# A gradient kernel on one core: part of the first tile loaded in separate pieces of 12 and 4 partitions

## The chip, the core and the metric

The kernel runs on one core of a Trainium2 chip; the other cores of the chip run nothing for it. The metric is the device time of one execution in microseconds (us), and the figure for a kernel is the median of its runs. The program is memory traffic with a little arithmetic: it reads 268.44 MB from the chip's main memory (HBM) and writes as much back. Between the two the data lie in the core's on-chip memory (SBUF), which has 128 partitions. Sixteen DMA engines move the data. VectorE (DVE) does the arithmetic, GpSimd (POOL) helps with the edges, and SyncE (SP) issues the transfers.

## What is computed

```python
def setup_inputs():
    return {"x": np.random.randn(8192, 8192).astype(np.float32)}

def reference(x):
    return np.gradient(x, axis=1)
```

Along each row of 8192 numbers, an inner element of the output is half the difference of its right and its left neighbour. The first element is x[1] - x[0] and the last is x[8191] - x[8190], both without the half.

## The kernel before

**Tiles.** `R = 2`, so one partition takes two consecutive rows, 2 x 8192 float32 numbers or 65,536 bytes that lie together in HBM. A tile is 128 partitions, or 256 rows and 8.39 MB, and there are `nsets = 32` tiles. `NB = 3` buffers called `slot0` to `slot2` hold tile i in slot i % 3. Each slot is 64 numbers (`SH`) longer than a tile: the load writes from column 64 on, and the result is written in place from column 0 on.

**One tile.** A load (line 60, one request of 128 x 16384 numbers) fills the slot. GpSimd computes the four edge differences of each partition into `ends` (line 70, 128 x 4). VectorE computes all inner differences in one instruction (line 76, 128 x 16382). The edges are then copied over the results (line 87), on GpSimd for tiles whose number leaves 1 or 3 when divided by 5, otherwise on VectorE. A store (line 89, again one request of 128 x 16384) writes the slot to HBM.

**Order.** The order is written out by hand. All 64 requests are issued by SP, one after the other: loads 0, 1, 2, then stores 0, 1, 2, loads 3, 4, 5, stores 3, 4, 5 and so on, to loads 30, 31, stores 30, 31. A store waits for the edge copy of its tile. Load i waits for the landing of store i - 3, which frees the slot. The function `chain` tells the framework that only these waits are needed. `loads` keeps the load instruction of each tile, so that the edge differences of tile i can be made to wait for it.

Of the kernel before, what the change touches and what calls it, by code (L numbers as in the profile page):

```python
# [1 line left out]

# [4 lines left out]


@with_exitstack
def kernel(  # L10
    ctx: ExitStack,
    tc: tile.TileContext,
    x: bass.AP,
    out: bass.AP,
):

    nc = tc.nc
    P = nc.NUM_PARTITIONS
    n, m = x.shape
    R = 2
    NB = 3  # L30
    SH = 64
    W = R * m
    nsets = n // (P * R)
    f32 = x.dtype

    x_sets = x.rearrange("(s p t) m -> s p (t m)", p=P, t=R)
    out_sets = out.rearrange("(s p t) m -> s p (t m)", p=P, t=R)

    pool = ctx.enter_context(tc.tile_pool(name="pool", bufs=1))
    slots = [pool.tile([P, SH + W], f32, name=f"slot{k}", tag=f"slot{k}") for k in range(NB)]  # L40
    ends = pool.tile([P, nsets, R, 2], f32, name="ends", tag="ends")
    loads, stores = [], [None] * nsets
    in_front = {}

    def chain(i, ins, *needed):

        group, engine = f"slot{i % NB}", ins.ins.engine
        keep = [o.ins for o in needed]  # L50
        if in_front.get(engine, (None,))[0] == group:
            keep.append(in_front[engine][1])
        tc.declare_no_dep(ins.ins, group=group, keep=keep, reason="implied by the needed step")
        tc.add_to_no_dep_group(group, ins.ins)
        in_front[engine] = group, ins.ins
        return ins

    def load(i):
        b = slots[i % NB]
        ins = nc.sync.dma_start(out=b[:, SH : SH + W], in_=x_sets[i])  # L60
        loads.append(chain(i, ins, *([stores[i - NB]] if i >= NB else [])))

    with tc.manual_schedule():
        for i in range(NB):
            load(i)
        for i in range(nsets):
            b = slots[i % NB]
            xin = b[:, SH : SH + W].rearrange("p (t m) -> p t m", m=m)

            ins = nc.gpsimd.tensor_sub(  # L70
                out=ends[:, i, :, :],
                in0=xin[:, :, 1 : m : m - 2],
                in1=xin[:, :, 0 : m - 1 : m - 2],
            )
            at = [chain(i, ins, loads[i])]
            ins = nc.vector._custom_dve(  # L76
                dve_ops.TENSOR_TENSOR_REDUCE_SUB_MAX,
                out=b[:, 1 : W - 1],
                in0=b[:, SH + 2 : SH + W],
                in1=b[:, SH : SH + W - 2],  # L80
                s0=0.0,
                s1=0.5,
            )
            halved = chain(i, ins, *at)
            res = b[:, 0:W].rearrange("p (t m) -> p t m", m=m)
            placer = nc.gpsimd if i % 5 in (1, 3) and i < nsets - 2 else nc.vector
            ins = placer.tensor_copy(out=res[:, :, 0 : m : m - 1], in_=ends[:, i, :, :])  # L87
            placed = chain(i, ins, halved)
            ins = nc.sync.dma_start(out=out_sets[i], in_=b[:, 0:W])
            stores[i] = chain(i, ins, placed)  # L90
            if i % NB == NB - 1:
                for k in range(i + 1, min(i + 1 + NB, nsets)):
                    load(k)


# [1 line left out]
_INS = ['x']  # L97
_OUTS = [((8192, 8192), 'float32')]


# [23 lines left out]
```

## Time and profile before

| | us |
|---|---|
| median of three runs | 1248.04 |
| lowest and highest of them | 1247.85, 1248.38 |
| span of the profiled execution, first to last instruction | 1245.7 |
| VectorE busy in it | 554.6 (45%) |
| GpSimd busy in it | 8.8 (1%) |

The profile is one execution. Its span leaves out what lies before the first and after the last instruction, which is why it is 2.3 us below the median of the runs. Three kinds of view are used here: the page's totals; the waits (which engine waited for what, and for how long in total); and a list of instructions in order of time, where a row of SP stands for a request that it issues and not for the transfer itself.

The trace also has a record of each packet that the DMA engines moved: its start, how long it took and how many bytes it had. There are 8192 data packets of 65,536 bytes, which is one partition of one tile each, and 1024 packets of 4 bytes, which tell the program that an engine has finished its part of a request. That is 128 data packets and 16 such marks for each of the 64 requests, so each engine moves 8 data packets and one mark per request. The records do not name the engine. Since a packet starts within a few ns of the end of the one before it on its engine, the sixteen streams can be followed as groups: the records in order of start, sixteen at a time, are called rounds here, and round 0 is the first packet of each engine.

### The profile page before, as it was taken

What the parts mean: (1) busy time and instruction counts of PE and PEld (TensorE: products, weight loads), DVE (VectorE), ACT (ScalarE), POOL (GpSimd) and SP (SyncE); (2) the same over time, 40 slices, a digit from 0 to 9 for tenths busy, and PEclk for the clock granted to TensorE, in tenths of its full rate; (3) what the DMA queues carried; (4) which work ended last, traced back from release to release, by engine and by line L of the source; (5) the groups of instructions that cost most, each with busy time, mean ns of one, the idle gap of its engine ahead of it and who ended that gap; (6) DMA issues with size and microseconds to landing.
All of it is one profiled execution on the core that took longest, in us unless ns stands there. A gap on an engine that the chain in (4) does not pass through costs nothing.

```text
span 1245.7 us, 237 instructions
## 1 busy us (share of the span) xinstructions
DVE 554.6 (45%) x52; POOL 8.8 (1%) x48
## 2 busy tenths in 40 slices
DVE  2850583069009702850582079009603840591083
POOL 0000000000000000000000000000000000000000
DMA  9999999999999999999999999999999999999999
GB/s 404 438 436 423 427 431 438 438 438 436 436 427 431 425 438 436 425 434 436 429 434 436 434 436 434 436 434 438 419 436 436 434 438 438 431 434 429 429 410 404
DMA packets 9217, 536.88 MB, mean 431 GB/s; under 512 B 1024, under 2 KB 1024, under 8 KB 1024
## 3 DMA queue, kind: packets, MB, share of 16 engines
q1 hardware_dynamic: 9216, 536.88, 99.8%
q14 instruction: 1, 0.01, 0.0%
HBM read 268.44 MB, written 268.44 MB: 431 GB/s over the span
## 4 chain that ended last, share of the span: by engine, by line
another core or an unknown queue 74%; DVE 18%; DMA 3%; issue 2%; POOL 1%; SPq 0%; POOLq 0%
DVE slot L76 18%; DMA slot<-in_x_dram 3%; POOL ends L70 0%; POOL slot L87 0%; SPq L60 0%; POOLq L119 0%; DVE slot L87 0%
## 5 line engine op out<-in xcount | busy, mean ns | idle before, releaser
L76 DVE CUSTOM_DVE_ANT_0 slot<-slot 128x16382 f32<-128x16382 f32 x32 | 551.2, 17224 | 668.7 <-POOL ends L70 668.7
L70 POOL TENSOR_TENSOR ends<-slot 128x4 f32<-128x4 f32 x32 | 6.3, 198 | 989.6 <-DMA slot<-in_x_dram 989.6
L87 POOL COPY slot<-ends 128x4 f32<-128x4 f32 x12 | 2.3, 190 | 207.9 <-DVE slot L76 207.9
L87 DVE COPY slot<-ends 128x4 f32<-128x4 f32 x20 | 3.4, 172 | 0.7
L108 POOL MEMSET const-bfloat16-1.0<- 128x1 bf16 x1 | 0.1, 101 | 0.0
L108 POOL MEMSET const-uint8-127<- 128x1 uint8 x1 | 0.1, 101 | 0.0
L108 POOL MEMSET const-float32-0.0<- 128x1 f32 x1 | 0.1, 98 | 0.2 <-issue 0.2
L108 POOL MEMSET const-float32-1.0<- 128x1 f32 x1 | 0.1, 98 | 0.0
## 6 DMA issues: line engine op xcount, KB each, us to landing
slot<-in_x_dram SPq DMA_DIRECT2D x32, 58.0
out_dram<-slot SPq DMA_DIRECT2D x32, 40.4
```

The lines of the kernel that those rows point to most:

```text
L70: ins = nc.gpsimd.tensor_sub(out=ends[:, i, :, :], in0=xin[:, :, 1 : m : m - 2], in1=xin[:, :, 0 : m - 1 : m - 2],)
L76: ins = nc.vector._custom_dve(dve_ops.TENSOR_TENSOR_REDUCE_SUB_MAX, out=b[:, 1 : W - 1], in0=b[:, SH + 2 : SH + W], in1=b[:, SH : SH + W - 2],
L87: ins = placer.tensor_copy(out=res[:, :, 0 : m : m - 1], in_=ends[:, i, :, :])
L108: nc = _bacc.Bacc("TRN2", target_bir_lowering=False, num_devices=1)
```

## The change

Of the first tile alone, the load is cut into four requests. All other loads, and all stores, stay as they are.

```diff
+    EVEN, CUT = P - 16, m - 2048
+
+    def parts_of(dram, i, sb, last):
+        whole = dram.rearrange("(s p t) m -> s p t m", p=P, t=R)[i]
+        rows = sb.rearrange("p (t m) -> p t m", m=m)
+        cuts = [(slice(EVEN, P), slice(0, CUT))]
+        first = EVEN
+        for k in last:
+            cuts.append((slice(first, first + k), slice(CUT, m)))
+            first += k
+        pairs = [(whole[p, :, c], rows[p, :, c]) for p, c in cuts]
+        pairs.insert(1, (dram.rearrange("(s p t) m -> s p (t m)", p=P, t=R)[i][0:EVEN], sb[0:EVEN]))
+        return pairs
...
     def load(i):
-        b = slots[i % NB]
-        ins = nc.sync.dma_start(out=b[:, SH : SH + W], in_=x_sets[i])
-        loads.append(chain(i, ins, *([stores[i - NB]] if i >= NB else [])))
+        sb = slots[i % NB][:, SH : SH + W]
+        after = [stores[i - NB]] if i >= NB else []
+        parts = parts_of(x, i, sb, (12, 4)) if i == 0 else [(x_sets[i], sb)]
+        loads.append(
+            [chain(i, nc.sync.dma_start(out=to, in_=of), *after) for of, to in parts]
+        )
...
-            at = [chain(i, ins, loads[i])]
+            at = [chain(i, ins, *loads[i])]
```

SP now issues for tile 0, in this order:

1. partitions 112 to 127, columns 0 to 6143 of each of their two rows (16 x 2 x 6144 numbers, pieces of 24,576 bytes);
2. partitions 0 to 111, whole (112 x 16384 numbers, pieces of 65,536 bytes);
3. partitions 112 to 123, columns 6144 to 8191 (12 x 2 x 2048 numbers, pieces of 8,192 bytes);
4. partitions 124 to 127, columns 6144 to 8191 (4 x 2 x 2048 numbers, pieces of 8,192 bytes).

Together they move the same 8.39 MB into the same places. The edge differences of tile 0 wait for all four. No other instruction of any engine changes its place; line numbers from there on are higher by five.

## The prediction

> **What bounds the kernel now.** I read the page's totals first, then the waits, then the list of instructions at both ends.
>
> ```profile
> span 1245.7 us, 237 instructions
> DVE 554.6 (45%) x52; POOL 8.8 (1%) x48
> DMA  9999999999999999999999999999999999999999
> DMA packets 9217, 536.88 MB, mean 431 GB/s; under 512 B 1024, under 2 KB 1024, under 8 KB 1024
> q1 hardware_dynamic: 9216, 536.88, 99.8%
> ```
>
> The DMA engines are busy in every slice, 99.8% of the span; VectorE works less than half of it. Of the 8192 data packets, median, 5th and 75th percentile all took 2418 ns, so one packet time is 2418 ns and the 512 packets of one engine need 1238.0 us. Only 7.7 us of the span are anything else.
>
> ```profile
> POOL ends L70 <- DMA slot<-in_x_dram: 989.6, 32, 77.4
> DVE slot L76 <- POOL ends L70: 668.7, 32, 60.2
> ...
> SPq L60 <- DMA out_dram<-slot: 373.1, 29, 19.3
> ```
>
> GpSimd waits for loads, VectorE for GpSimd, and SP, before a load, for the store that frees the slot. Nothing here waits for arithmetic at the DMA's cost, as the two ends show:
>
> ```profile
> 0.74 1.33 SPq L60 DMA_DIRECT2D slot<-in_x_dram  x3
> 22.71 0.20 POOL L70 TENSOR_TENSOR ends<-slot 128x4 f32<-128x4 f32 x1 [22.27 <-DMA slot<-in_x_dram]
> 22.95 17.22 DVE L76 CUSTOM_DVE_ANT_0 slot<-slot 128x16382 f32<-128x16382 f32 x1 [22.95 <-POOL ends L70]
> 40.20 0.17 DVE L87 COPY slot<-ends 128x4 f32<-128x4 f32 x1
> 40.40 40.06 SPq L89 DMA_DIRECT2D out_dram<-slot  x3
> ...
> 1187.17 17.22 DVE L76 CUSTOM_DVE_ANT_0 slot<-slot 128x16382 f32<-128x16382 f32 x1 [59.84 <-POOL ends L70]
> 1204.42 0.17 DVE L87 COPY slot<-ends 128x4 f32<-128x4 f32 x1
> 1204.62 19.69 SPq L89 DMA_DIRECT2D out_dram<-slot  x2
> 1206.28 0.20 POOL L70 TENSOR_TENSOR ends<-slot 128x4 f32<-128x4 f32 x1 [19.14 <-DMA slot<-in_x_dram]
> ```
>
> Store 0 is issued at 40.40 us, but load 2 keeps the engines until 60.4 or later (its last packets begin at 57.95 to 58.54): 20 us of cover. At the end there is none. Tile 30's arithmetic starts when the slowest engine has landed load 30 (round 488, which follows it, begins at 1183.62 us on the fastest engine and at 1185.92 on the slowest), store 30 follows 17.5 us later, and all engines start it together (round 496, 1205.47 to 1205.84). So the end is set by **the slowest of sixteen engines**: a delay of the fast ones costs nothing there, a delay of the slowest moves the end one for one.
>
> What made that engine slow? Its second packet began at 5.39 us; 487 more would have put it at 1182.96, and it was 2.96 us later. The losses lie almost all in one place: the last packet of a load before the engines turn to stores. At the first turn the sixteen packets took 3162 to 3819 ns, 1.10 us over the usual on average (17.6 us summed over 16). The nine later turns cost 0.01 to 0.63 us on average, mean 0.23. Meanwhile the engines drift apart, from 0.6 us at the start to 2.3 near the end.
>
> **The change part by part.** *Issuing.* SP issues six requests at the start instead of three, three more at 0.34 us (median of 339 ns): load 1 leaves SP about 1.0 us later. Its packets are due at 21.7 us, so some 18 us of cover remain; without it the cost would be 1.0 us. The first request starts as before, 1.0 us after issue, and has 48 KB for each engine, 1.8 us at the usual rate; the second is issued 0.42 us after it and arrives before that is done. *Waits.* The edge differences of tile 0 wait for four landings instead of one; behind them on GpSimd is tile 1's, behind those VectorE, behind it store 0 with its 20 us. SP's requests take completion semaphores in turn, and three more requests shift that turn; what a later request then waits for is a request eight places earlier, long landed. I price both at nothing.
>
> *More and smaller packets.* One whole partition per engine becomes pieces of 24 and 8 KB, with 32 more marks, two per engine at 9 ns: 0.02 us. A start-up cost per new request is between nothing (queued packets follow each other within a few ns) and 0.60 us, the mean excess of the very first packets: for the three added requests 0 to 1.8 us. The queued packets are nearer, so 0.
>
> *Unequal shares.* A partition's last 2048 columns of two rows are 16 KB, a quarter of a packet: 0.60 us. If 12 engines take one partition each of request 3 and four of those again one of request 4, four engines carry 0.60 us more than before and four 0.60 less. If request 4 falls on the four left out, all shares are equal and this is 0. I take +0.60 on the slowest. [...]
>
> *Crowding.* Before, each request spreads 16 engines over 128 partitions. Now request 1 puts all sixteen into 16 neighbouring partitions, request 3 twelve into 12, request 4 four into 4, and request 2's seven partitions per engine no longer divide as eight do. No row shows so narrow a request. From below the cost is 0: all packets keep their rate. From above I let the whole first tile, eight packet times, go at the pace of the worst packet in the trace: 8 x (3819 - 2418) = 11.2 us. The first turn is the one place where all sixteen engines are seen in each other's way while they write SBUF; I hold that nearer than undisturbed streaming, and take its mean: 8 x 1.10 = **+8.8 us**. Nothing hides it, since the engines have no idle time to lend and each later request queues behind. [...]
>
> *The first turn.* Engines that are further apart could be spared part of it. From nothing to all of the slowest engine's 2.96 us; I take the first turn falling to the mean of the others, 1.10 - 0.23 = -0.9.
>
> Sum: 0.60 + 8.8 - 0.9 = +8.5 us. Span 1245.7 + 8.5 = 1254.2; with the 2.3 us between span and median, **1256.5 us**. Upper end: 0.60 + 11.2 + 1.8 = +13.6, 1261.6; with crowding at half my value, +4.1 or 1252.1. That is the likeliest case's own range.
>
> **The rivals.** *Only the shares count.* Narrow requests run at full rate, and the slowest engine carries 0.60 us more, or 0 if shares come out equal: 1248.0 to 1248.6, less up to 0.9 at the first turn. For it: ordinary packets keep to 2418 ns within a few ns through nearly all of the trace. Against: they do so with every engine on its own eight of 128 partitions.
>
> *The stagger pays, faster.* Place: the turns from loads to stores. The first cost 1.10 us with the engines 0.6 us apart; the turn at 291 us, with 1.2 us between them, 0.08, and the one at 988 us, with 2.4, 0.01. A spread of 1.2 us or more from the start could spare the slowest engine up to 2.96 us, less whatever extra share it has: 1245.1, or 1245.7 with the full share. It decides if crowding costs less than it spares; below 2.96 - 0.60 = 2.4 us it wins. Against: the turn at 522 us cost 0.63 with the engines 1.8 us apart, so spread alone does not spare a turn.
>
> *A starved start.* If the four requests come too slowly from SP, all engines idle up to 1.0 us between them: 1249.0. The 1.8 us of work in request 1 speaks against it.
>
> **How the numbers follow.** Crowding 0.70, at 1256.5. Shares only, with the starved start, 0.18, around 1248.5. Stagger 0.12, around 1245.5. What this kernel's measurement tells from no change is about 0.2%, 2.5 us: below 1245.5 or above 1250.5. Crowding gives slower but for 0.02; shares only gives no change; of the stagger 0.09 lies beyond the bound, where nearly all turns are spared. So slower 0.68, same 0.23, faster 0.09. The range for 8 in 10 starts at 1247.0, which leaves out the stagger, and ends at 1262.0, just over the upper sum.
>
> **What would show it.** The packets of q1 should number 9296 (48 more data packets, 32 more marks). Right, if the first edge difference starts near 32 us instead of 22.71, tile 0's pieces run far above the time for their bytes, and the 9 us last to the end of the trace. Only the shares, if it starts near 23.5 and the sixteen packet streams are 1.2 us apart with all turns as before. Stagger, if the first turn's excess falls from 1.10 below 0.3 and round 488's slowest start comes before 1185.9. I am wrong above all if narrow requests run at full rate: then 8.8 us of my sum are not there.

## The result, and the profile after

The changed kernel takes 1268.18 us (1267.89 to 1268.99) against 1248.04 for the kernel before, measured beside it: a ratio of 1.0162, 95% interval 1.0149 to 1.0174. It is 20.1 us slower. I had forecast slower, 1256.5 us, with 1262.0 as the upper end. The direction and its cause were right, and the size was less than half of what it is.

The page of the changed kernel, first its totals and then the three lines of its transfer list that stand for requests 1, 3 and 4 of tile 0 (kilobytes, and where it is given the us from issue to landing; request 2 is counted with the other loads):

```profile
span 1266.4 us, 245 instructions
DVE 554.6 (44%) x52; POOL 8.9 (1%) x48
DMA  9999999999999999999999999999999999999999
GB/s 219 337 433 431 431 435 428 437 441 431 439 433 433 431 431 433 437 424 447 431 439 435 431 431 428 433 433 445 433 433 437 428 433 435 433 431 443 433 391 397
DMA packets 9297, 536.88 MB, mean 424 GB/s; under 512 B 1056, under 2 KB 1056, under 8 KB 1056
q1 hardware_dynamic: 9296, 536.88, 99.6%
...
slot<-in_x_dram SPq DMA_DIRECT2D x1, 768.0 KB, 9.9
...
slot<-in_x_dram SPq DMA_DIRECT2D x1, 192.0 KB
slot<-in_x_dram SPq DMA_DIRECT2D x1, 64.0 KB
```

The busy row is the same as before, nines throughout: the engines are occupied all the time. The row of GB/s tells what that hides. Each slice is 31.7 us; the first moves data at half the later rate (219 GB/s against 433), the second at three quarters (337), and from the third on the kernel runs as before. A packet counts as busy for as long as it takes, so the slice at 219 GB/s shows the same nine as those at 433. The packets number 9296, as worked out, and 99.6% of the engines' time went into them.

The same stretches in both kernels, before and then after (start and end of the stretch, its length, VectorE's and GpSimd's busy time, the clock, the DMA's busy share, GB/s; a packet is counted whole where it starts, so short stretches are rough):

```profile
0.00:10.00 10.00, 0.00 (x0) 0.20 (x4) 1.00 0.98 400
10.00:40.00 30.00, 17.05 (x1) 0.20 (x1) 1.00 0.98 426
40.00:46.00 6.00, 4.07 (x3) 0.20 (x1) 1.00 0.88 382
...
62.00:100.00 38.00, 17.40 (x2) 0.20 (x1) 1.00 0.96 416
```

```profile
0.00:10.00 10.00, 0.00 (x0) 0.20 (x4) 1.00 1.15 184
10.00:40.00 30.00, 0.00 (x0) 0.00 (x0) 1.00 0.94 223
40.00:46.00 6.00, 0.00 (x0) 0.00 (x0) 1.00 0.88 259
...
62.00:100.00 38.00, 34.26 (x4) 0.59 (x3) 1.00 1.01 436
```

Request 2, the 112 whole partitions, fills the stretch from 10 to 40 us at 223 GB/s. The rows of the instructions in order of time show where that goes:

```profile
0.73 4.06 SPq L65 DMA_DIRECT2D slot<-in_x_dram  x6
46.15 0.20 POOL L75 TENSOR_TENSOR ends<-slot 128x4 f32<-128x4 f32 x1 [45.70 <-DMA slot<-in_x_dram]
...
65.16 0.20 POOL L75 TENSOR_TENSOR ends<-slot 128x4 f32<-128x4 f32 x1 [18.81 <-DMA slot<-in_x_dram]
...
84.51 0.20 POOL L75 TENSOR_TENSOR ends<-slot 128x4 f32<-128x4 f32 x1 [1.64 <-DMA slot<-in_x_dram]
...
1207.51 0.20 POOL L75 TENSOR_TENSOR ends<-slot 128x4 f32<-128x4 f32 x1 [77.08 <-DMA slot<-in_x_dram]
```

Each row of GpSimd starts 0.07 to 0.16 us after the last mark of a load has landed (45.99, 65.09, 84.44 and 1207.44 us): loads 0, 1, 2 and 30. Before, load 0's row stood at 22.71 us, and these are the other three:

```profile
42.04 0.20 POOL L70 TENSOR_TENSOR ends<-slot 128x4 f32<-128x4 f32 x1 [19.13 <-DMA slot<-in_x_dram]
...
62.44 0.20 POOL L70 TENSOR_TENSOR ends<-slot 128x4 f32<-128x4 f32 x1 [2.69 <-DMA slot<-in_x_dram]
...
1186.93 0.20 POOL L70 TENSOR_TENSOR ends<-slot 128x4 f32<-128x4 f32 x1 [77.07 <-DMA slot<-in_x_dram]
```

So the kernel is 23.4 us late after load 0, 23.1 after load 1, 22.1 after load 2 and 20.6 at load 30. Nothing more is lost after load 0 has landed; on the contrary, 1.0 us comes back at the first turn from loads to stores and 1.5 us after it. The span grew by 20.7 us.

The packet records give the rates. Typical ones of the changed kernel's first tile:

```
request 1, second pieces (24,576 bytes):    about 3600 ns each, usual rate 907 ns
request 2, first three packets (65,536):    about 4770 ns each after the start, usual rate 2418 ns
request 2, fourth and fifth:                about 3050 and 3560 ns on most engines
request 2, sixth and seventh:               about 4550 and 4770 ns, the last up to 5529
requests 3 and 4 (8,192 bytes):             600 to 1010 ns each, usual rate 302 ns
```

Sixteen engines at 24,576 bytes in 3600 ns are 109 GB/s, a quarter of the usual 434 (65,536 bytes in 2418 ns). Request 1 lasted from 2.26 to 9.3 us, request 2 from there to between 38.6 and 41.9 us, engine by engine. The first packets of load 1 that start beside the tail are slow too, up to 6033 ns.

### The profile page after: what moved, and what is told of

It is laid out like the page before. It is cut to its first block, busy times and chain, and to the rows that moved or that the text cites. A ratio compares the mean times of both kernels' runs of the same rounds, so it can differ in the third digit from the quotient of the medians.

```text
span 1266.4 us, 245 instructions
## 1 busy us (share of the span) xinstructions
DVE 554.6 (44%) x52; POOL 8.9 (1%) x48
## 3 DMA queue, kind: packets, MB, share of 16 engines
q1 hardware_dynamic: 9296, 536.88, 99.6%
## 4 chain that ended last, share of the span: by engine, by line
another core or an unknown queue 74%; DVE 18%; DMA 3%; issue 2%; POOL 1%; SPq 0%; POOLq 0%
DVE slot L81 18%; DMA slot<-in_x_dram 3%; POOL ends L75 0%; POOL slot L92 0%; SPq L65 0%; POOLq L124 0%; DVE slot L92 0%; POOLq L75 0%
```

## The experiments

Two theories stood against each other. **Crowding:** the set of partitions that a request covers sets its rate. **Pieces:** the number of requests and the small pieces cost. A third, **shares,** puts the loss on the unequal shares. In all the kernels below only tile 0 is loaded otherwise, unless said; the edits are shortened, with numbers in place of names, and a line without a condition holds for tile 0 alone.

**Whole partitions in two requests** (112 to 127, then 0 to 111):

```diff
-        parts = parts_of(x, i, sb, (12, 4)) if i == 0 else [(x_sets[i], sb)]
+        parts = [(x_sets[i][112:128], sb[112:128]), (x_sets[i][0:112], sb[0:112])] if i == 0 else [(x_sets[i], sb)]
```

> Tile 0 is loaded in two requests of whole partitions, 112 to 127 and then 0 to 111: no column cut, equal shares. Theory (which partitions a request covers sets its rate, as in the changed kernel, where 16 partitions went at 109 GB/s and 112 began at 220): 1.05 MB at 109 GB/s is 9.6 us instead of 2.4, and 112 partitions again need some 30 us instead of 17, so the first edge difference starts at 42 to 47 us and the time is 1263 to 1269 us. Rival (small pieces and the number of requests): there are none here but one request more, so it starts before 25 us and the time is within 2 us of the kernel before.

Measured: 1268.53 us, ratio 1.0162 (1.0142 to 1.0182); tile 1's edge difference at 62.90 us, and the first one here:

```profile
43.92 0.20 POOL L83 TENSOR_TENSOR ends<-slot 128x4 f32<-128x4 f32 x1 [43.48 <-DMA slot<-in_x_dram]
```

There are no small pieces and no unequal shares here, and the time is that of the changed kernel; at load 1, 20.9 of its 23.1 us are there. Pieces and shares are out as its main cause.

**More pieces over all partitions:**

```diff
+        parts = [(x_sets[i][:, c:d], sb[:, c:d]) for c, d in [(0, 6144), (6144, 8192), (8192, 14336), (14336, 16384)]]
```

> Tile 0 is loaded in four requests that each cover all 128 partitions: pieces of 24 and 8 KB by columns, more small pieces than in the changed kernel, equal shares. Theory (partitions covered): full rate, the first edge difference starts at 22.7 to 24 us, time within 1.5 us of the kernel before, the first turn still costs about 1 us per engine. Rival (small pieces and requests): much of the 20 us, over 1255 us.

Measured: 1248.50 us, ratio 1.000 (0.9991 to 1.0010). Its first rows:

```profile
22.78 0.20 POOL L82 TENSOR_TENSOR ends<-slot 128x4 f32<-128x4 f32 x1 [22.34 <-DMA slot<-in_x_dram]
...
42.04 0.20 POOL L82 TENSOR_TENSOR ends<-slot 128x4 f32<-128x4 f32 x1 [19.07 <-DMA slot<-in_x_dram]
```

Four requests with 512 pieces of 24 and 8 KB land tile 0 within 0.1 us of one request. With every request over all 128 partitions, the cut cost 0.0 us at load 1, which stands at 42.04 us in both kernels. The first turn cost 1.09 us per engine, as in the kernel before.

**Two halves of 64 partitions:**

```diff
+        parts = [(x_sets[i][0:64], sb[0:64]), (x_sets[i][64:128], sb[64:128])]
```

> Tile 0 is loaded in two requests of 64 whole partitions each, both with equal shares and large pieces. Theory: each half runs at about 220 GB/s, so the tile takes 38 us instead of 19.3, the first edge difference starts near 41.5 us, time 1264 to 1268 us. Rival that only awkward divisions (112, 12, 4) are slow: no change, 1247 to 1249 us.

Measured: 1267.82 us, ratio 1.0156 (1.0136 to 1.0177), with the first edge difference at 44.15 us:

```profile
44.15 0.20 POOL L83 TENSOR_TENSOR ends<-slot 128x4 f32<-128x4 f32 x1 [43.71 <-DMA slot<-in_x_dram]
```

Nothing divides awkwardly here, and it is as slow as the changed kernel. So it is not the odd numbers 112, 12 and 4.

**The disputed cost by itself.** The kernel before, with nine extra loads ahead of it into the third buffer, one after the other; their data are loaded again by the ordinary load 2. Each entry gives the first partition, the end and the step:

```diff
+        probes = [probe(*p) for p in [(0, 128, 1), (0, 16, 1), (0, 64, 4), (0, 128, 8), (0, 32, 1), (0, 128, 4), (0, 64, 1), (0, 112, 1), (0, 96, 1)]]
```

> Before the first tile, nine extra loads of whole partitions (65,536 bytes each) into a buffer, each waiting for the one before: 128 partitions; 16 neighbours; 16 in steps of 4; 16 in steps of 8; 32 neighbours; 32 in steps of 4; 64; 112; 96 neighbours. Theory (places decide): packets take 2.42 us in the 128, about 9.6 us for 16 neighbours, about 4.8 us for 16 in steps of 4 or of 8, for 32 and for 64; 112 starts at 4.8 us per packet. Rival (only the number of partitions decides): the three kinds of 16 take the same time. Rival (no such limit on an idle machine): 2.4 us everywhere. The time is longer by the sum of the extra loads, 110 to 160 us by the theory.

Measured in one run: 1401.42 us. The stretches from issue to issue of the first eight, in the order of the list (same columns as above; each holds about 2 us of waiting for the landing):

```profile
0.73:22.59 21.86, 0.00 (x0) 0.00 (x0) 1.00 0.92 384
22.59:34.22 11.63, 0.00 (x0) 0.00 (x0) 1.00 0.75 90
34.22:41.60 7.38, 0.00 (x0) 0.00 (x0) 1.00 0.65 142
41.60:49.42 7.82, 0.00 (x0) 0.00 (x0) 1.00 0.62 134
49.42:61.79 12.37, 0.00 (x0) 0.00 (x0) 1.00 0.81 170
61.79:69.45 7.66, 0.00 (x0) 0.00 (x0) 1.00 0.71 274
69.45:92.24 22.79, 0.00 (x0) 0.00 (x0) 1.00 0.88 184
92.24:125.71 33.47, 0.00 (x0) 0.00 (x0) 1.00 0.92 219
```

The second, third and fourth row move the same 1.05 MB on 16 partitions. Sixteen neighbours take 11.63 us, sixteen in steps of 4 or 8 only 7.38 and 7.82. The fifth and sixth row move the same 2.1 MB: 32 neighbours take 12.37 us, 32 in steps of 4 take 7.66. From the first packet's start to the last one's end the rates are:

| partitions | GB/s | median packet, ns |
|---|---|---|
| 128 | 409 | 2419 |
| 16 neighbours | 107 | 8678 |
| 16 in steps of 4 | 190 | 4721 |
| 16 in steps of 8 | 178 | 4822 |
| 32 neighbours | 198 | 5117 |
| 32 in steps of 4 | 348 | 2474 |
| 64 neighbours | 202 | 5119 |
| 112 neighbours | 230 | 4681 |
| 96 neighbours | 206 | 5005 |

Both rivals fall: neither the number of partitions alone decides (16 of them ran at 107, 190 and 178 GB/s), nor is the limit missing on an idle machine (409 GB/s on 128, but 230 on 112). What decides is which partitions a request covers: 32 in steps of 4 ran at 348 GB/s, 32 neighbours at 198. More neighbours help little from there on: 64 ran at 202, 96 at 206, 112 at 230. Why, no run here shows. In every kernel here a partition also stands for its own stretch of 65,536 bytes in HBM, so the runs alone do not tell whether the crowding lies on the SBUF side or on the HBM side.

**Equal shares in the tail** (16 partitions in one request in place of 12 and 4):

```diff
-        parts = parts_of(x, i, sb, (12, 4)) if i == 0 else [(x_sets[i], sb)]
+        parts = parts_of(x, i, sb, (16,)) if i == 0 else [(x_sets[i], sb)]
```

> As the changed kernel, but the last 2048 columns of partitions 112 to 127 come in one request of 16 instead of 12 and 4, so shares are equal. Theory (crowding makes nearly all of the loss): load 0 lands at 44 to 47 us as in the changed kernel, time within 2 us of its 1268.2. Rival (unequal shares are what costs): the time falls by more than 3 us. If the larger distance between the engines spared the later turns, this kernel's slowest engine loses 2.5 us between load 2 and load 30, as in the kernel before, and not 1.0 as in the changed one.

Measured: 1267.70 us, ratio 1.0161 (1.0147 to 1.0175). Tile 1's edge difference:

```profile
63.43 0.20 POOL L75 TENSOR_TENSOR ends<-slot 128x4 f32<-128x4 f32 x1 [18.83 <-DMA slot<-in_x_dram]
```

It came at 65.16 in the changed kernel, so 12 and 4 cost 1.7 us more than 16 at that point. At load 30 the order is reversed in the profiles, 1208.25 against 1207.51; but the profiled run of this kernel was the slowest of its four, at 1269.02 us, and by the medians it is not the slower one. Between load 2 and load 30 its slowest engine lost 3.5 us. (That loss is the time between the two edge differences, less 58 requests of 8 packets at 2418 ns, 1121.95 us.)

**The narrow tail alone** (a wide request for three quarters of the tile):

```diff
+        parts = [(x_sets[i][p, c], sb[p, c]) for p, c in [(slice(0, 128), slice(0, 12288)), (slice(0, 112), slice(12288, 16384)), (slice(112, 124), slice(12288, 16384)), (slice(124, 128), slice(12288, 16384))]]
```

> Tile 0: the first 12288 numbers of all 128 partitions in one request, then the last 4096 (16 KB) of partitions 0 to 111, 112 to 123 and 124 to 127 apart. A quarter of the changed kernel's crowded bytes, the same unequal shares and the same number of requests. Theory: 1.8 MB of 112 partitions at 230 GB/s is 8.0 us instead of 4.2, the 12 and the 4 add 1 to 3.6 us, so load 0 lands 5 to 7.5 us later than in the kernel before, time 1251 to 1256 us. Rival (requests that leave out partitions cost by themselves, whatever their bytes): 1262 us or more.

Measured: 1253.38 us, ratio 1.0045 (1.0031 to 1.0058), with the first edge difference 7.5 us later than before and tile 1's 7.2 later:

```profile
30.20 0.20 POOL L82 TENSOR_TENSOR ends<-slot 128x4 f32<-128x4 f32 x1 [29.76 <-DMA slot<-in_x_dram]
```

A quarter of the crowded bytes costs about a third of the changed kernel's 23.1 us. With four requests in both, the loss went with the crowded bytes here, not with the requests.

**Unequal shares without neighbours:**

```diff
+        parts = [(x_sets[i][r:128:4], sb[r:128:4]) for r in range(3)] + [
+            (x_sets[i][3:128:4, 0:12288], sb[3:128:4, 0:12288]),
+            (x_sets[i][3:96:4, 12288:16384], sb[3:96:4, 12288:16384]),
+            (x_sets[i][99:128:4, 12288:16384], sb[99:128:4, 12288:16384])]
```

> Tile 0 in six requests of 32 partitions in steps of 4 (the kind that ran at full rate in the measurement of nine loads), of which the last 16 KB of every fourth partition are cut into 24 and 8 partitions, so that shares are unequal without neighbours being crowded. Theory: load 0 lands 0 to 3 us later than the 22.6 us of the kernel before, first packets of each request near 2.4 us; time 1247 to 1251 us. Rival (any cut of the partitions is slow): 1260 us or more. If unequal shares alone are worth something, it is below 1247.

Measured: 1248.87 us, ratio 1.0008 (0.9999 to 1.0017). Its rows for loads 0, 1, 2 and 30:

```profile
25.59 0.20 POOL L85 TENSOR_TENSOR ends<-slot 128x4 f32<-128x4 f32 x1 [25.14 <-DMA slot<-in_x_dram]
...
44.66 0.20 POOL L85 TENSOR_TENSOR ends<-slot 128x4 f32<-128x4 f32 x1 [18.88 <-DMA slot<-in_x_dram]
...
64.01 0.20 POOL L85 TENSOR_TENSOR ends<-slot 128x4 f32<-128x4 f32 x1 [1.64 <-DMA slot<-in_x_dram]
...
1187.71 0.20 POOL L85 TENSOR_TENSOR ends<-slot 128x4 f32<-128x4 f32 x1 [77.10 <-DMA slot<-in_x_dram]
```

It is 2.6 us late at load 1, 1.6 at load 2 and 0.8 at load 30: of the 2.6 us, 1.8 come back. After the first packets of the kernel, the requests of 32 in steps of 4 ran at 2418 ns a packet. This is the change's idea without its neighbours, and it is a draw, not a gain.

**Why the first turn was free.** In the kernel before, the engines lose 1.10 us each when they first turn from loads to stores; in the kernels with a slow tile 0 they lose nothing there (0.00 to 0.01 us).

```diff
+        probes = [probe(*p) for p in [(0, 128, 1)]]
```

> The kernel before with one more full load of 128 partitions in front, into the third buffer, which is loaded again later: all else is 19.3 us later. It asks why the first turn to stores cost 1.1 us per engine in the kernel before and nothing in those with a slow first tile. If it is the engines' distance, or the slow tile itself, the first turn still costs about 1.1 us here and the time is 1248.2 + 19.3 + 0 = 1267.5 us. If it is that the first turn comes early after the start, it costs under 0.3 us and the time is about 1266.5 us.

Measured in one run: 1267.57 us, and the first turn cost 0.83 us. That it comes early after the start is not the reason.

```diff
+        parts = [(x_sets[i][r:128:4], sb[r:128:4]) for r in range(4)]
```

> Tile 0 in four requests of 32 whole partitions in steps of 4, equal shares, no column cut. If the first turn is spared because engines are at unequal distances (2.2 us apart with the unequal shares in steps of 4), it costs about 1.1 us per engine here, since the engines stay 0.5 to 0.8 us apart, and the time is within 0.6 us of the kernel before. If any division other than one request of 128 spares it, it costs under 0.1 us and the time is about 1247.0 us.

Measured: 1248.39 us, ratio 1.0006 (0.9997 to 1.0015), first turn 0.89 us, with the engines 0.9 us apart at load 1. It is 0.6 us late at load 1, so 2.0 of the 2.6 us of the unequal cut in steps of 4 belong to its tail. Cutting the tile in steps of 4 does not spare the turn, while the same cut with unequal shares, 2.2 us apart, did.

The two kernels as they are, profiled a second time:

> The changed kernel, profiled a second time. If what it gives back between load 2 and load 30 belongs to the change, the slowest engine loses about 1.0 us there again, the first turn is free again and load 30 lands 20 to 21 us later than in the kernel before; if it was chance, that loss lies anywhere between 1.0 and 3.1 us.

> The kernel before, profiled a second time. If its first turn belongs to it, it costs about 1.1 us per engine again, and the slowest engine loses about 2.5 us between load 2 and load 30; if these were chance, the first turn differs by more than 0.3 us.

Measured: the changed kernel, 1268.27 us, with load 1's edge difference at 65.00 us and load 30's at 1207.18; the kernel before, 1247.95 us, with a first turn of 1.05 us. Side by side, the slowest engine's loss between load 2 and load 30:

| kernel | shares in tile 0 | loss, us |
|---|---|---|
| before, twice | equal | 2.5, 2.9 |
| nine extra loads ahead | equal | 2.5 |
| one extra load ahead | equal | 3.2 |
| two whole requests | equal | 2.8 |
| four by columns | equal | 3.1 |
| two halves | equal | 2.6 |
| equal tail of 16 | equal | 3.5 |
| steps of 4, equal | equal | 2.5 |
| changed kernel, twice | unequal | 1.0, 0.9 |
| wide body, narrow tail | unequal | 1.6 |
| steps of 4, unequal | unequal | 1.7 |

Each figure is one profile, and the runs of the kernel before alone lie more than 2 us apart (1246.58 to 1249.32). Still every kernel with unequal shares lost less than every one with equal shares, and the changed kernel did so twice: on its slowest engine the unequal shares go with 1 to 2 us less. Whether they spare turns is not shown. Averaged over the sixteen engines, the nine later turns cost about as much in the kernel of two whole requests (equal, about 1.0 us in all) as in the changed one; it may also be that the same losses fall on engines that are ahead. For the first turn the distance between the engines is not the whole story: the two halves left them only 0.3 us apart at loads 1 and 2 and still turned free. Nor is a slow tile 0: after the nine extra loads, tile 0 came in one ordinary request, the engines were 0.9 us apart as with the equal steps of 4, and that turn was free. What decides it stays open; it was not pursued, since it is 1 us of 20.

## Why the prediction was wrong

*The bound.* Right. The end is set by the slowest DMA engine, and a delay in tile 0 goes through to the end: 23.1 us at load 1, 20.6 at load 30, 20.7 in the span. No wait on an engine took part.

*Issuing and waits.* Priced at nothing. No wait shows in the result, but the price of issuing was off. Six requests took SP 4.06 us instead of my 2.4, and the first request's packets began at 2.26 us instead of 1.75, so 0.5 us of the start was not covered. It shows between two kernels with equal shares: 63.43 us at load 1 with the equal tail, whose packets also began at 2.25, against 62.90 with two whole requests, which began at 1.76.

*More and smaller packets.* Right: 9296 packets, and four requests over all partitions cost 0.0 us at load 1.

*Unequal shares, +0.60.* The marks show that they are unequal: request 3 has 12 landings and request 4 has 4, and the sixteen landings of load 1 behind them come in groups of four, eight and four, at 62.33 to 62.54, 62.99 to 63.51 and 63.67 to 65.09 us. Four packets of load 1 begin at 39.52 to 39.80 us, on engines that carried none of the small pieces. Against an equal tail they cost 1.7 us at load 1 instead of 0.60. These pieces are crowded too, 600 to 1010 ns for what usually takes 302, which would account for it.

***Crowding, +8.8: the step that failed.*** That requests of neighbouring partitions run slower was right, and the term was mis-sized. Without unequal shares or a column cut it measured +20.9 us at load 1, 2.6 us for each of the eight packet times that I had priced at 1.10; the first edge difference, forecast near 32 us, started at 46.15. I had taken the mean loss of the packets at the first turn as the pace of a crowded tile, and the worst of them as its upper end. The records show only that those packets took 3162 to 3819 ns; that the engines are in each other's way there was my reading, and no run shows it. Both figures come from requests that cover all 128 partitions; they are no measure of a kind of request that the trace did not hold, and 11.2 us was no upper end. Request 1 lasted 7.0 us instead of the 1.8 at the usual rate. Request 2, the 112 whole partitions, ran at 223 to 230 GB/s and needed some 31 us instead of the 16.9 that seven packets take, 14 us of the loss. My sum did count request 2, seven of the eight packet times, but at 7.7 us for the 14 that it lost.

*The first turn, -0.9.* It went from 1.10 us to nothing, so -1.0 for the landing; and I had only that turn in the sum, while the stretch from there to load 30 gave 1.5 us more, 2.5 in all. One reading behind this term was off: the rounds put the slowest engine's end of load 30 at 1185.92 us, 2.3 us after the fastest one's, but the marks of load 30 landed from 1183.84 to 1186.87, 3.0 us apart. Engines more than one packet time of 2418 ns apart fall into different rounds, so near the end of the trace rounds mix them up, and the slowest engine had lost more than the 2.96 us that I took as the bound. The sum did not use that bound.

The sum by what was measured, from load 1 on: +20.9 for two crowded requests, +2.2 more for the late start (0.5) and the unequal tail (1.7), -1.0 at the first turn, -1.5 from there on: 20.6 at load 30.

*The rivals.* Shares only gave 1248.5 us, and the unequal shares in steps of 4, in which no request holds neighbouring partitions, measured 1248.87: that rival would have been right for a kernel that cut its tile in another way. Of stagger's two signs one came true, a first turn below 0.3 us, and 2.5 us came back up to load 30; that the distance between the engines does it is not shown. It lost to the price, since crowding was far above the 2.4 us at which it would have won. The starved start did not show: the packets of request 2 follow those of request 1 within 3 ns, and only the first request began 0.5 us late.

## What to carry to other kernels

When a load is cut by partitions, price each new request by which partitions it covers, the largest request first (112 whole partitions made 14 of the 23.1 us here): 112 of 128 neighbours ran at about half the rate of all 128, 230 GB/s against 409. Cut by columns instead (0.0 us at load 1 here), or take partitions in steps of 4 (32 of them ran at 2418 ns a packet, and the whole tile so cut was 0.6 us late). The busy share, 99.6% here against 99.8% before, does not show such a loss; the GB/s beside it do, 219 against 404 in the first slice.

## What was not expected of the hardware

Leaving out an eighth of the partitions nearly halved the rate: against 409 GB/s on 128, 112 neighbours at 230 are hardly faster than 64 at 202, or 32 at 198. How a request of 112 is divided among the engines is not in the records, so why it does so badly stays open. And in kernels whose unequal shares left the engines 1.8 to 3.0 us apart after the first tile, the slowest engine lost about 1.5 us less over the next 1100 us; how, is not shown.
